# Modulation columns summed as a row and turned by transfers over HBM, residuals issued earlier, side work held back at group ends

## The chip, the cores and the metric

One core of a Trainium2 chip runs the whole kernel. The metric is the device time of one execution in microseconds. A core has a matrix engine (TensorE, PE in the profile), a vector engine (VectorE, DVE), an activation engine (ScalarE, ACT), GpSimd (POOL), and SyncE (SP), whose queue issues all the transfers of this kernel. Matmul results land in eight PSUM banks of 128 x 512 floats; everything else lives in SBUF, and HBM holds inputs and outputs.

## The reference

One layer of a decoder trunk on x (512 tokens x 1024), in float32: a modulation vector from c, two sparse attention mixers on a shared projection, a gated merge, an output projection, and a SwiGLU block.

```python
mod = jax.nn.silu(c) @ w_mod[l] + b_mod[l]
sh_m, sc_m, gt_m, sh_f, sc_f, gt_f = [m[:, None, :] for m in jnp.split(mod, N_MOD, axis=-1)]
h = rms_norm(x, g_mix_norm[l]) * (1.0 + sc_m) + sh_m
proj = h @ w_in[l]
...
o_a = dsa_attention(q_a, k_a, v_a, q_i, k_i, w_i)
...
o_b = moba_attention(q_b, k_b, v_b)
merged = (jax.nn.sigmoid(gate_a) * (o_a @ w_br_dsa[l])
          + jax.nn.sigmoid(gate_b) * (o_b @ w_br_moba[l]))
x = x + gt_m * (merged @ w_out[l])
h = rms_norm(x, g_ffn_norm[l]) * (1.0 + sc_f) + sh_f
g_ff, u_ff = jnp.split(h @ w_gate_up[l], 2, axis=-1)
x = x + gt_f * ((jax.nn.silu(g_ff) * u_ff) @ w_down[l])
```

The change concerns `sh_f` and `sc_f`, 1024 values each, which are needed with the channel on the partition (as columns), and the order of work around `x + gt_m * (merged @ w_out)`.

## The kernel before, in words

Every large product is done as three passes of a split weight and a split activation (high x high, high x low, low x high; `mm3`), so each weight tile `st` that arrives from HBM is cast by ACT to `wh`, and DVE forms `wl` = `st` - `wh`. Projections are done in groups: `group` cuts a 1024 x 512 weight block into four chunks; four PSUM banks (`psacc`) are filled over all chunks, and the last chunk's unit (`last`) goes bank by bank, so that each finished bank can be emptied (`fin`) while PE fills the others. These matmuls are the main work.

All else is side work: generators that are run between the main matmuls. It holds the norm, rotation and transposing of queries and keys (`post`), the index scores (`index_queries`: two matmuls per head into `pss` or `pspv`, a relu by ACT into a tile `s`, and DVE's weighing of it into `score`), the top-k rounds (`topk`), the attention heads (`head`), and the rest of the modulation vector (`columns_task`, `rows_task`, `gtf_task`).

No hardware decides the order. While the program is written out, `Clocks` keeps an estimated time for each engine and the time at which each tile is ready, from a cost formula. After each main triple, `main3` calls `step`, which advances each side task whose inputs are ready on these clocks and whose engines lead PE by less than the task's `slack`. The order so found is fixed in each engine's instruction stream, and every engine runs its stream strictly in order. For transfers, `arriving` sets a tile ready 2.0 after `ck.dma`, a running sum of transfer sizes that a transfer moves up only by its own size or to the tile's last use, not to the engines' present time. All operations are issued through one recorder (`Noted`), so the profile gives line 107 for all of them and tells them apart by tile names.

The second half of the modulation vector is made in `columns_task` (line 924): four parts of 512 columns, each by `mod_columns` (line 894). `column_sums` loads two 1 MB tiles `K` of `w_mod` and adds the eight row blocks, each times one column of silu(c), on DVE (`K<-K,cs`). `halves` splits the 128 x 512 sum into `gu` high (ACT) and low (DVE). Then the sum over partitions is taken on PE as eight matmuls that each move two columns of ones against a 128 x 128 block of the sums, so that it lands as columns, and DVE adds the bias from PSUM into `mcol` (lines 901 to 905). `mod_rows` (line 908) makes other parts as rows with two 512-column matmuls. `mcol` is first read at the end of `columns_task` and then in `norm_task`, past 400 us.

`out_units` (line 1111) does the second half of the output projection, token tile by token tile. After the last k of a tile, `main3` calls `step` before the residual (`s<-psacc,cg`, then `V<-V,s`) is issued and the bank is released. `merge` (line 981) joins the two gated branches. `prep` (line 522) casts a chunk's weights as soon as DVE's clock allows.

Of the kernel before, what the change touches and what calls it, by code (L numbers as in the profile page):

```python
# [25 lines left out]
P = 128  # L26
# [87 lines left out]
def layer(ctx, tc, x, vecs, w_mod, w_in, gvecs, w_br_dsa, w_br_moba, w_out, w_gate_up, w_down, cosh, sinh, cosi, sini, out):  # L114
# [6 lines left out]
    wp = ctx.enter_context(tc.tile_pool(name="wp", bufs=3))  # L121
    sm = ctx.enter_context(tc.tile_pool(name="sm", bufs=2))
    pp = ctx.enter_context(tc.tile_pool(name="pp", bufs=1, space=PS))

    NB = {"H": 4, "O": 4, "K": 4, "V": 2, "g": 16, "gu": 2, "s": 3, "pT": 2, "cg": 2}
    uid = [0]
# [15 lines left out]
    def done(*tiles):  # L142
        for tile in tiles:
            name = tile.tensor.name
            free[tag_of.pop(name)].append(ck.last[name][0])
# [12 lines left out]
    def ps(tag, shape=(P, 512), dt=F32):  # L158
        uid[0] += 1
        return taken("ps" + tag, pp.tile(list(shape), dt, name=f"ps{tag}_{uid[0]}", tag="ps" + tag, bufs=NPB[tag]))  # L160
# [266 lines left out]
    def room(tag, n=1):  # L427
        return lambda: sorted(free[tag])[n - 1] if len(free[tag]) >= n else None
# [9 lines left out]
    def spawn(gen, slack=2.0, rank=2, on=busy):  # L438
        tasks.append([gen, (), slack, on, rank])
        tasks.sort(key=lambda task: task[4])  # L440

    def step():

        moved = False
        while True:
            hit = False
            for wait in (0.0, 0.15):
                for task in list(tasks):
                    fill = task[4] == 3
                    if wait and (hit or not fill):  # L450
                        continue
                    while task in tasks:
                        now = ck.at[PE]
                        if max(ck.at[e] for e in task[3]) > now + task[2]:
                            break
                        limit = max(now, ck.at[DVE] + 0.12 + wait) if fill else now
                        if not all(w is not None and w <= limit for w in map(when, task[1])):
                            break
                        hit = True
                        try:  # L460
                            task[1] = next(task[0]) or ()
                            if not isinstance(task[1], tuple):
                                task[1] = (task[1],)
                        except StopIteration:
                            tasks.remove(task)
                        if fill:
                            break
            if not hit:
                return moved
            moved = True  # L470
# [21 lines left out]
    def group(srcs, n, accs_of, mm, order, fin, need=(), change=None):  # L492

        accs = {}
        nk = 2 * len(srcs)
        chunks = []
        for c, src in enumerate(srcs):
            def unit(w, ks, js, last, c=c):
                if not accs:
                    accs.update(accs_of())  # L500
                for a, b in ([(k, j) for j in js for k in ks] if last else [(k, j) for k in ks for j in js]):
                    mm(accs[b], w[0][:, a], w[1][:, a], 2 * c + a, b, c == 0 and a == 0, 2 * c + a == nk - 1)
                    if last and a == ks[-1]:
                        fin(b, accs[b])
                        done(accs[b])

            last = c == len(srcs) - 1
            h = (len(order) + 1) // 2
            parts = [((0, 1), order[:h]), ((0, 1), order[h:])] if last else [((0,), order), ((1,), order)]
            units = [lambda w, p=p, unit=unit, last=last: unit(w, p[0], p[1], last) for p in parts]  # L510
            chunks.append((lambda src=src, n=n: wload(src, 2, n), units, need, change))
        return chunks

    def drive(chunks, ws, ahead=2):
        sts = {}

        def load(c):
            if c < len(chunks) and chunks[c][0]:
                need_room("st")
                sts[c] = chunks[c][0]()  # L520

        def prep(c):
            if c < len(chunks) and chunks[c][0]:
                st = sts.pop(c)
                if chunks[c][3]:
                    chunks[c][3](st)
                uid[0] += 1
                h, l = [wp.tile(list(st.shape), F32R, name=f"w{q}_{uid[0]}", tag="w" + q) for q in "hl"]
                se.copy(h, st)
                yield h  # L530
                ve.tensor_tensor(out=l, in0=st, in1=h.bitcast(F32), op=ALU.subtract)
                done(st)
                ws[c] = h, l
            load(c + 1)

        load(ahead)
        for c, (load_of, units, need, _) in enumerate(chunks):
            pump(lambda: all(f in ready for f in need) and (not load_of or c in ws))
            for u, unit in enumerate(units):
                unit(ws.get(c))  # L540
                if u == 0:
                    spawn(prep(c + ahead), slack=4.0, rank=-1, on=(DVE,))
                    step()
            ws.pop(c, None)
# [339 lines left out]
    def halves(sums):  # L884

        yield room("gu", 2)
        hi, lo = (t("gu", [P, 512], F32R) for _ in range(2))
        yield sums
        se.copy(hi, sums)
        yield hi  # L890
        ve.tensor_tensor(out=lo, in0=sums, in1=hi.bitcast(F32), op=ALU.subtract)
        return hi, lo

    def mod_columns(col0):

        tile, sums = yield from column_sums(col0, "K")
        parts = yield from halves(sums)
        done(tile)
        yield parts + (room("pstr"),)
        pc = ps("tr", (P, 4, 2))  # L900
        for j in range(4):
            for n, part in enumerate(parts):
                te.matmul(pc[:, j, :], part[:, j * P:(j + 1) * P], oner.to_broadcast([P, 2]), start=n == 0, stop=n == 1)
        j0 = col0 // P
        ve.tensor_tensor(out=mcol[:, j0:j0 + 4], in0=pc[:, :, 0], in1=bm[:, j0:j0 + 4], op=ALU.add)
        done(pc, *parts)

    def mod_rows(acc, col0, tag):

# [57 lines left out]
    def br_done(br, half):  # L967
        def fin(f, acc):
            if not br and not half and not f:
                pump(lambda: len(free["K"]) == 4)  # L970
                merged.extend(t("K", [P, 4, S], F32R) for _ in range(4))
            j = 8 * br + 4 * half + f
            pump(lambda: f"gate{j}" in ready)
            ve.tensor_tensor(out=gates[j], in0=acc, in1=gates[j], op=ALU.mult)
            if not br:
                spawn(merge(half, f), slack=0.5, rank=0)
            if half and f == 3:
                done(*outs[br])
        return fin

    def merge(half, f):
        g, gb = gates[4 * half + f], gates[8 + 4 * half + f]
        ve.tensor_tensor(out=g, in0=g, in1=gb, op=ALU.add)
        yield g
        hi, lo = merged[half][:, f, :], merged[2 + half][:, f, :]
        se.copy(hi, g)
        yield hi
        ve.tensor_tensor(out=lo, in0=g, in1=hi.bitcast(F32), op=ALU.subtract)
        done(g, gb)
        ready.add(f"m{half}{f}")  # L990
        if all(f"m{a}{b}" in ready for a in range(2) for b in range(4)):
            ready.add("merged")
# [118 lines left out]
    def out_units():  # L1111
        units = []
        accs = {}
        for i in range(NT):
            for k2 in range(NK // 2):
                def unit(_, i=i, k2=k2):
                    if not i and not k2:
                        h2.extend(t("H", [P, 4, S], F32R) for _ in range(4))
                    if not k2:
                        need_room("psacc")  # L1120
                        accs[i] = ps("acc")
                    for k in (2 * k2, 2 * k2 + 1):
                        mh, ml = mk(k, i)
                        pump(lambda: len(wo) > k)
                        main3(accs[i], mh, ml, wo[k][0][:, 0], wo[k][1][:, 0], k == 0, k == NK - 1)
                    if k2 == NK // 2 - 1:
                        spawn(norm_task(i, residual(accs[i], gtm, i, 1)), slack=4.0, rank=-0.1 * i)
                        done(accs[i])
                        if i == NT - 1:
                            done(*gtm, *(q for hl in wo for q in hl), *merged)  # L1130
                units.append(unit)
        return units

# [198 lines left out]
```

## Time and profile before

| | |
|---|---|
| device time, three runs | 796.37, 797.54, 798.59 us (median 797.54) |
| profiled execution | 798.46 us |
| its span, first to last instruction | 796.4 us |
| instructions | 10056 |
| PE busy | 780.6 us, 98% |
| DVE busy | 475.6 us, 60% |
| ACT busy | 364.0 us, 46% |
| POOL busy | 28.4 us, 4% |
| HBM | 125 GB/s over the span |

Shares are of the span. An average over the whole span hides that DVE's and ACT's work lies mostly before 300 us. A row of a timeline gives start, duration, engine, operation, result <- operands, shape, count and, in brackets, the idle time ahead of it with what ended it. PE's durations overlap, since matmuls are pipelined: the time that one takes from the engine is the distance between starts, not the duration shown.

### The profile page before, as it was taken

The page shows a single profiled execution, that of the slowest core. Times are in us where ns is not written, and L with a number is a line of the kernel's source. Part 1 is how long each engine was busy: PE and PEld are TensorE (multiplying, and loading weights), DVE is VectorE, ACT ScalarE, POOL GpSimd, SP SyncE. Part 2 cuts the span into 40 slices and gives each one's busy share as a digit, 9 for nine tenths or more (in the row PEclk, how much of TensorE's full clock was granted, in tenths as well). Part 3 has the DMA queues.
Part 4 walks back from the last instruction along what each step waited for, and adds up shares of the span by engine and source line. Part 5 has one row for each costly group of instructions (what it writes and reads, how often), then busy time and mean ns, then how long its engine had stood idle before and what let it go on. Part 6 is the DMA issues. An engine that isn't in the chain of part 4 may idle for free.

```text
span 796.4 us, 10056 instructions
## 1 busy us (share of the span) xinstructions
PE 780.6 (98%) x3733; PEld 647.3 (81%) x3733; DVE 475.6 (60%) x873; ACT 364.0 (46%) x763; POOL 28.4 (4%) x32
## 2 busy tenths in 40 slices
PE   5999999999999999999999999999999999999998
PEld 4887788787788788888888988888888888888886
DVE  3974979998799638538857365333333333644542
ACT  5763579898566777334534323223322322211210
POOL 1000012110010000000000000000000000000000
PEclk8899999999999999999999999999999999999999
DMA  9946443321144444634520166332332322433411
GB/s 309 356 138 225 126 158 83 129 75 58 54 132 137 155 136 155 212 105 139 178 82 15 40 210 212 106 106 87 99 105 85 101 85 74 133 106 110 128 53 53
DMA packets 78036, 100.59 MB, mean 126 GB/s; under 512 B 5980, under 2 KB 46244, under 8 KB 77988
## 3 DMA queue, kind: packets, MB, share of 16 engines
q1 hardware_dynamic: 77988, 99.96, 39.7%
q8 instruction: 29, 0.48, 0.2%
q14 instruction: 19, 0.16, 0.1%
HBM read 97.85 MB, written 2.10 MB: 125 GB/s over the span
## 4 chain that ended last, share of the span: by engine, by line
PE 95%; ACT 2%; DVE 1%; DMA 1%; issue 0%; SPq 0%; POOL 0%; DVEq 0%; ACTq 0%
PE psacc L107 61%; PE pstr L107 16%; PE pspv L107 9%; PE pss L107 9%; DMA O<-in_x_dram 1%; ACT sqj L107 0%; ACT V L107 0%; DVE wl L107 0%; DVE score L107 0%; ACT g L107 0%; ACT s L107 0%; DVE O L107 0%; DVE pT L107 0%; DVE s L107 0%; POOL m L107 0%
## 5 line engine op out<-in xcount | busy, mean ns | idle before, releaser
L107 DVE TENSOR_TENSOR wl<-st,wh 128x1024 fp32r<-128x1024 f32 (+1 forms) x119 | 144.9, 1217 | 123.3 <-ACT wh L107 123.1
L107 ACT CAST wh<-st 128x1024 fp32r<-128x1024 f32 (+1 forms) x119 | 124.3, 1045 | 179.8 <-PE psacc L107 66.7
L107 PE MATMUL psacc<-H,wh 128*128 128x512 f32 x576 | 181.9, 397 | 0.0
L107 PE MATMUL psacc<-wh,H 128*128 128x512 f32 x384 | 131.1, 409 | 2.2 <-ACT H L107 1.3
L107 PEld LDWEIGHTS psacc<-H,wh 128*128 128x128 f32 x576 | 106.8, 188 | 23.0 <-issue 1.4
L107 PE MATMUL psacc<-H,wl 128*128 128x512 f32 x288 | 112.4, 390 | 0.0
L107 PEld LDWEIGHTS psacc<-wh,H 128*128 128x128 f32 x384 | 72.4, 189 | 19.4 <-ACT H L107 1.4
L107 PE MATMUL psacc<-wl,H 128*128 128x512 f32 x192 | 71.6, 394 | 0.0
L107 PEld LDWEIGHTS psacc<-H,wl 128*128 128x128 f32 x288 | 54.1, 188 | 11.5
L107 PE MATMUL pstr<-H,wh 128*128 128x512 f32 (+1 forms) x176 | 54.3, 390 | 0.0
L107 PEld LDWEIGHTS psacc<-wl,H 128*128 128x128 f32 x192 | 36.6, 191 | 7.7 <-issue 1.0
L107 POOL TENSOR_TENSOR m<-m,mhalf 128x4 f32<-128x4 f32 (+1 forms) x24 | 26.6, 1108 | 404.6 <-DVE m L107 357.0
L107 PE MATMUL psacc<-wh,K 128*128 128x512 f32 x128 | 39.8, 389 | 0.0
L107 PE MATMUL psacc<-O,wh 128*128 128x512 f32 x128 | 39.4, 389 | 0.0
L107 PEld LDWEIGHTS pstr<-H,wh 128*128 128x128 f32 (+1 forms) x176 | 32.3, 183 | 7.7
L107 ACT ACTIVATE s<-s,att 128x128 f32<-128x128 f32 (+3 forms) x64 | 34.1, 560 | 2.4 <-DVE att L107 2.4
L107 PE MATMUL pstr<-H,wl 128*128 128x512 f32 (+1 forms) x88 | 34.3, 390 | 0.0
L107 DVE TENSOR_TENSOR s<-psacc,s 128x512 f32<-128x512 f32 x12 | 8.3, 692 | 41.1 <-PE psacc L107 38.9
L107 PEld LDWEIGHTS psacc<-wh,K 128*128 128x128 f32 x128 | 24.0, 188 | 5.2 <-DVE g L107 0.2
L107 PEld LDWEIGHTS psacc<-O,wh 128*128 128x128 f32 x128 | 24.0, 188 | 5.0
L107 PEld LDWEIGHTS pspv<-pT,V 128*128 128x128 f32 x160 | 21.9, 190 | 6.4 <-DVE O L107 3.0
L107 DVE TENSOR_TENSOR st<-st,cg 128x1024 f32<-128x1024 f32 x22 | 26.8, 1219 | 0.0
(232 smaller groups left out, 1339.6 us busy)
## 6 DMA issues: line engine op xcount, KB each, us to landing
st<-in_w_gate_up_dram SPq DMA_DIRECT2D x88, 256.0 KB, 3.2
st<-in_w_in_dram SPq DMA_DIRECT2D x36, 512.0 KB, 3.6
K<-in_w_mod_dram SPq DMA_DIRECT2D x12, 1024.0 KB, 5.9
st<-in_w_down_dram SPq DMA_DIRECT2D x22, 512.0 KB, 3.6
K<-in_w_mod_dram SPq DMA_DIRECT2D x16, 512.0 KB, 6.2
st<-in_w_in_dram SPq DMA_DIRECT2D x16, 256.0 KB, 4.2
st<-in_w_mod_dram SPq DMA_DIRECT2D x8, 512.0 KB, 3.9
O<-in_x_dram SPq DMA_DIRECT2D x4, 512.0 KB, 5.4
```

The source lines that it names most:

```text
L107: inst = f(*args, **kw)
```

## The change

`mod_columns` takes the sum over partitions as a row: two matmuls with 512 moving columns and a two-column stationary of ones, a copy of the row by ACT into the sums' tile, a transfer of the row to HBM, a second transfer from there into four columns of `mcol`, and then the bias in place on DVE. `held_back` takes 1.0 from the lead that side work may have while the last chunk of a group is worked. `merge` gets a slack larger by 1.0. `prep` waits on the clocks for its load's planned arrival before the cast. In `out_units` the last triple of a token tile is no longer followed by `step`; that comes after the residual.

```diff
     def step():
...
-                        if max(ck.at[e] for e in task[3]) > now + task[2]:
+                        if max(ck.at[e] for e in task[3]) > now + task[2] - held_back[0]:
                             break
...
             def unit(w, ks, js, last, c=c):
                 if not accs:
                     accs.update(accs_of())
+
+                held_back[0] = 1.0 if last else 0.0
...
                 if chunks[c][3]:
                     chunks[c][3](st)
+                yield st
...
     def mod_columns(col0):

         tile, sums = yield from column_sums(col0, "K")
-        parts = yield from halves(sums)
+        hi, lo = yield from halves(sums)
+        yield hi, lo, room("pstr")
+        pc = ps("tr", (2, 512))
+        te.matmul(pc, oner.to_broadcast([P, 2]), hi, start=True, stop=False)
+        te.matmul(pc, oner.to_broadcast([P, 2]), lo, start=False, stop=True)
+        done(hi, lo)
+        yield pc
+        row = sums[0:1, :]
+        se.copy(row, pc[0:1, :])
+        done(pc)
+        yield sums
+        j0 = col0 // P
+        turned = dp.tile([1, 512], F32, name=f"turned{j0}")
+        nc.sync.dma_start(turned, row)
+        nc.sync.dma_start(mcol[:, j0:j0 + 4], turned.rearrange("o (a p) -> p (o a)", p=P), allow_slow_non_contiguous=True)
+        arriving(mcol, 512)
+        yield mcol
+        ve.tensor_tensor(out=mcol[:, j0:j0 + 4], in0=mcol[:, j0:j0 + 4], in1=bm[:, j0:j0 + 4], op=ALU.add)
         done(tile)
-        yield parts + (room("pstr"),)
-        pc = ps("tr", (P, 4, 2))
-        for j in range(4):
-            for n, part in enumerate(parts):
-                te.matmul(pc[:, j, :], part[:, j * P:(j + 1) * P], oner.to_broadcast([P, 2]), start=n == 0, stop=n == 1)
-        j0 = col0 // P
-        ve.tensor_tensor(out=mcol[:, j0:j0 + 4], in0=pc[:, :, 0], in1=bm[:, j0:j0 + 4], op=ALU.add)
-        done(pc, *parts)
...
-                spawn(merge(half, f), slack=0.5, rank=0)
+                spawn(merge(half, f), slack=1.5, rank=0)
...
-                        main3(accs[i], mh, ml, wo[k][0][:, 0], wo[k][1][:, 0], k == 0, k == NK - 1)
+
+                        (mm3 if k == NK - 1 else main3)(accs[i], mh, ml, wo[k][0][:, 0], wo[k][1][:, 0], k == 0, k == NK - 1)
                     if k2 == NK // 2 - 1:
                         spawn(norm_task(i, residual(accs[i], gtm, i, 1)), slack=4.0, rank=-0.1 * i)
                         done(accs[i])
                         if i == NT - 1:
                             done(*gtm, *(q for hl in wo for q in hl), *merged)
+                        step()
```

What this does to the streams is seen in three places. Numbers behind a name count allocations and differ between the kernels. On DVE, at the first of the four parts of the modulation columns, the stream of before is:

```order
L107 TENSOR_TENSOR wl_977<-st_941,wh_976 128x1024
L107 TENSOR_TENSOR gu_983<-K_858,gu_982 128x512
L107 TENSOR_TENSOR mcol<-pstr_1030,cols 128x4
L107 TENSOR_SCALAR score_991<-s_995,wi 128x256
L107 SCALAR_TENSOR_TENSOR score_991<-s_1000,wi,score_991 128x256
L107 TENSOR_TENSOR gu_1065<-g_663,cg_685 128x4x64 x2
```

and the stream of the change is:

```order
L107 TENSOR_TENSOR gu_1068<-K_855,gu_1067 128x512
L107 TENSOR_TENSOR wl_1074<-st_1032,wh_1073 128x1024
L107 SCALAR_TENSOR_TENSOR score_990<-s_1088,wi,score_990 128x256
L107 SCALAR_TENSOR_TENSOR score_990<-s_1094,wi,score_990 128x256
L107 TENSOR_TENSOR gu_1140<-g_667,cg_687 128x4x64 x2
L107 TENSOR_TENSOR mcol<-mcol,cols 128x4
L107 TENSOR_SCALAR K_1178<-K_1178,cs 128x512
L107 SCALAR_TENSOR_TENSOR K_1178<-K_1178,cs 128x512 x3
L107 SCALAR_TENSOR_TENSOR K_1180<-K_1180,cs,K_1178 128x512
L107 SCALAR_TENSOR_TENSOR K_1180<-K_1180,cs 128x512
L107 SCALAR_TENSOR_TENSOR score_990<-s_1127,wi,score_990 128x256
L107 SCALAR_TENSOR_TENSOR score_990<-s_1133,wi,score_990 128x256
```

The bias add now takes `mcol` itself, and behind it stand six products of the next part's sums and then the weighing of the next two index heads (`s_1127` and `s_1133`).

On ACT, around the row copy of the same part (the copy to one partition, `1x512`), the change has:

```order
L107 ACTIVATE g_665<-g_665,m_4_159_1025 128x128 x4
L107 ACTIVATE s_1127<-pss_1124 128x256
L107 ACTIVATE s_1133<-pspv_1130 128x256
L107 ACTIVATE sqj,m_4_180_1135<-g_667 128x128 x4
L107 COPY K_855<-pstr_1120 1x512
L107 COPY g_1150<-psacc_868 128x512
```

The relus of the two index heads and four squares of a norm stand ahead of it, and the emptying of the next group's first bank behind it.

On SP, the only queue that issues transfers, the change has at that place:

```order
L858 DMA K_1178<-in_w_mod_dram 128x4x512
L858 DMA K_1180<-in_w_mod_dram 128x4x512
L916 DMA turned_1174<-K_855 1x512
L180 DMA st_1305<-in_w_in_dram 128x2x512
L917 DMA mcol<-turned_1174 128x4x1
L180 DMA st_1371<-in_w_in_dram 128x2x512
```

A weight load now stands between the two new transfers, and the next weight load stands behind both.

On DVE, at the last token tile of the output projection (`s<-psacc,cg` is the residual's product, `V<-V,s` its sum, `pT<-pstr,acol,mcol` the modulation of a transposed token tile), before:

```order
L107 TENSOR_SCALAR pT_4142<-pstr_4137,acol,mcol 128x128 x4
L107 TENSOR_TENSOR s_4147<-psacc_4069,cg_3301 128x512
L107 TENSOR_TENSOR V_3116<-V_3116,s_4147 128x512
L107 TENSOR_TENSOR H_3934<-pT_4132,H_3932 128x4x128
L107 TENSOR_SCALAR m_1_801_4177<-ss_656 128x1
```

and in the change:

```order
L107 TENSOR_TENSOR s_4121<-psacc_4063,cg_3131 128x512
L107 TENSOR_TENSOR V_3242<-V_3242,s_4121 128x512
L107 TENSOR_SCALAR pT_4139<-pstr_4134,acol,mcol 128x128 x4
L107 TENSOR_SCALAR m_1_801_4172<-ss_658 128x1
L107 TENSOR_TENSOR H_3924<-pT_4129,H_3922 128x4x128
```

The residual, which releases the bank, now stands ahead of the four modulations.

## Rows read from the trace of the kernel before

**Rows 1.** The page, busy time of the engines over the span.

```profile
PE 780.6 (98%) x3733; PEld 647.3 (81%) x3733; DVE 475.6 (60%) x873; ACT 364.0 (46%) x763; POOL 28.4 (4%) x32
```

**Rows 2.** Waits of PE: us in total, times, longest.

```profile
PE psacc L107 <- DVE s L107: 1.0, 1, 1.0
PE psacc L107 <- ACT g L107: 0.8, 1, 0.8
```

**Rows 3.** Busy by stretch: length; PE, PEld, DVE, ACT, POOL, PEclk, DMA share, GB/s.

```profile
100.00:150.00 50.00, 49.96 (x262) 42.45 (x261) 45.28 (x94) 42.29 (x125) 10.53 (x7) 1.00 0.36 117
...
500.00:790.00 290.00, 290.00 (x1281) 240.15 (x1280) 113.23 (x112) 72.49 (x85) 0.00 (x0) 1.00 0.31 94
```

**Rows 4.** Timeline of PE: start, us, operation, around modulation matmuls.

```profile
107.34 1.15 PE L107 MATMUL pstr<-oner,gu 128*128 128x2 f32 x8
108.35 0.48 PE L107 MATMUL pspv<-O 128*128 128x256 f32 x2
...
159.01 1.03 PE L107 MATMUL pstr<-oner,gu 128*128 128x2 f32 x8
159.91 0.48 PE L107 MATMUL psacc<-wh,H 128*128 128x512 f32 x1
...
160.69 0.38 PE L107 MATMUL pss<-K,K 128*128 128x128 f32 x2
...
320.00 0.63 PE L107 MATMUL pstr<-gu,oner 128*128 128x512 f32 x2
320.47 0.62 PE L107 MATMUL psacc<-H,wh 128*128 128x512 f32 x2
```

**Rows 5.** Timeline of ACT and of PE where a bank copy is late.

```profile
151.83 1.30 ACT L107 ACTIVATE g<-g,m 128x128 f32<-128x128 f32 x4
153.01 0.62 ACT L107 CAST gu<-K 128x512 fp32r<-128x512 f32 x1
153.52 1.09 ACT L107 COPY g<-psacc 128x512 f32<-128x512 f32 x2
...
154.17 0.50 PE L107 MATMUL psacc<-wh,H 128*128 128x512 f32 x1 [0.75 <-ACT g L107]
```

**Rows 6.** Timeline of DVE and of PE where a residual is late.

```profile
429.37 1.37 DVE L107 TENSOR_SCALAR pT<-pstr,acol,mcol 128x128 f32<-128x128 f32 x4 [1.36 <-PE pstr L107]
...
431.39 1.81 PE L107 MATMUL psacc<-H,O 128*128 128x256 f32 x13 [0.99 <-DVE s L107]
```

**Rows 7.** Groups of ACT by shape: busy, mean ns.

```profile
L107 ACT ACTIVATE sqj<-g 128x128 f32<-128x128 f32 x64 | 19.9, 311 | 2.9 <-DVE m L107 1.3
...
L107 ACT ACTIVATION_READ_ACCUMULATOR sqj<-g 128x1 f32 x64 | 12.0, 188 | 0.0
```

**Rows 8.** DMA issues: KB each, median us to landing.

```profile
st<-in_w_in_dram SPq DMA_DIRECT2D x36, 512.0 KB, 3.6
...
st<-in_w_in_dram SPq DMA_DIRECT2D x1, 288.0 KB, 3.1
...
out_dram<-V SPq DMA_DIRECT2D x2, 128.0 KB, 1.7
```

**Rows 9.** Groups of DVE by shape: busy, mean ns.

```profile
L107 DVE TENSOR_TENSOR wl<-st,wh 128x1024 fp32r<-128x1024 f32 x118 | 144.1, 1221 | 123.3 <-ACT wh L107 123.1 <-DMA st<-in_w_in_dram 0.3
...
L107 DVE SCALAR_TENSOR_TENSOR K<-K,cs 128x512 f32<-128x512 f32 x24 | 17.9, 748 | 0.4
...
L107 DVE SCALAR_TENSOR_TENSOR score<-s,wi,score 128x256 f32<-128x256 f32 x7 | 3.4, 482 | 0.3
```

**Rows 10.** Waits of DVE between 80 and 440 us.

```profile
DVE mcol L107 <- PE pstr L107: 2.7, 4, 1.0
DVE cg L107 <- DMA cg<-in_vecs_dram: 1.8, 1, 1.8
```

**Rows 11.** Busy by stretch, the start of the span, columns as in Rows 3.

```profile
2.40:13.40 11.00, 4.85 (x26) 4.05 (x27) 4.29 (x12) 5.95 (x13) 2.25 (x5) 1.00 1.00 342
13.40:23.70 10.30, 8.99 (x36) 7.53 (x35) 5.78 (x15) 6.92 (x13) 0.00 (x0) 0.51 1.12 359
```

More of the change, by code (lines that the diff above doesn't have):

```diff
@@ L123, in layer @@
     pp = ctx.enter_context(tc.tile_pool(name="pp", bufs=1, space=PS))
+    dp = ctx.enter_context(tc.tile_pool(name="dp", bufs=1, space=bass.MemoryType.DRAM))
     NB = {"H": 4, "O": 4, "K": 4, "V": 2, "g": 16, "gu": 2, "s": 3, "pT": 2, "cg": 2}
@@ L440, in spawn @@
         tasks.sort(key=lambda task: task[4])
+    held_back = [0.0]
     def step():
```

## The prediction

> **What bounds the kernel now.** I read the busy times first: PE works 98% of the span [rows 1], so a time saved elsewhere counts only where PE would else wait, and a PE instruction saved counts in full. PE's waits on side work are short [rows 2]: one for a residual (1.0 us), one for a bank copy (0.8 us). The stretches then show where new waits could come from. From 500 us on PE runs 1281 matmuls in 290 us, 0.226 us each, with DVE busy for 113 us; between 100 and 150 us, where the first modulation columns are made, DVE is busy for 45.28 of 50 us and ACT for 42.29 [rows 3]. So a late DVE has some 4.7 us of idle time in 50 to catch up with, less in any one microsecond. Times below are against the profiled execution, 798.46 us (span 796.4 and 2.1 around it), which is 0.9 above the median 797.54.
>
> **The change part by part: gains.** The eight two-column matmuls of a modulation part took 1.01 us from one start to the next operation's start at 107.34, and 0.90 at 159.01; the pair of 512-column matmuls of `mod_rows`, the new form, took 0.47 at 320.00 [rows 4]. Four parts: 4 x (0.955 - 0.47) = **-1.9**.
>
> The residual: at 429.37 DVE starts four modulations, 1.37 us, and only then the residual that frees PE's next bank; PE idles for 0.99 us [rows 6]. With the residual first, the wait goes: its operands were there, and what is late next, the four modulations, feeds the same tile's H, far from the next matmul. With 0.1 for the slower first matmul behind a wait, **-1.1**.
>
> The smaller lead while a group is emptied: at 151.83 ACT does four scalings (1.18 to the next start) and a cast (0.51) ahead of the copy that frees a bank, and PE idles for 0.75 us [rows 5]. With less side work ahead, **-0.9** with 0.1 for the first matmul, which shows 0.50 there. No other PE wait has this form [rows 2]. The larger slack of `merge` restores its lead inside such groups, and the wait of `prep` for a planned arrival costs nothing: a weight load lands in 3.6 us [rows 8] and is issued two chunks ahead.
>
> **Losses.** Side matmuls now come in some 100 stretches between main ones instead of 92 (counted in PE's stream). Three main matmuls between side work took 0.78 us, 159.91 to 160.69 [rows 4], 0.10 more than three at 0.226. Eight more stretches: **+0.7** (0 to 0.8).
>
> **The wait of the bias add** is the largest term. DVE runs in order, and its add now waits for ACT's row copy and for two transfers in series, with six products and the index weighings queued behind it. Let X be the start of the first part's pair on PE. *Until the row is copied:* ACT does four scalings (1.18, as in [rows 5]), two relus of half a bank (0.4 each, from half the 0.54 per copy of [rows 5] and a start), four squares with their accumulator reads, 4 x (0.31 + 0.19) = 2.0 [rows 7], and the copy (0.54): X + 4.5. *The transfers, T:* the trace has none of 2 KB. The nearest are a store of 128 KB, 1.7 us, and a load in 288-byte pieces, 3.1 us [rows 8]; the second new transfer moves 512 pieces of four bytes. I take 1.7 + 3.1 = 4.8. At least it is 1.7 twice, 3.4. At most the second runs behind the weight load issued between them (3.6) and then takes its own 3.1: 6.7. The add comes at X + 9.3. *Behind it:* six products, at most 6 x 0.75 = 4.5; the first is a plain scaling, so I count 4.2; one weighing, 0.48 [rows 9]; then ACT's relu of the next head, 0.5, which needs the tile that this weighing frees; X + 14.5. The relu frees the PSUM bank of a later index matmul. *PE gets there at:* in its stream stand the pair (0.47), 36 main matmuls at 0.226 (8.1), and five index products of two matmuls each, three over 256 columns and two over 384, with four transposes (by columns at the same pace, 1.9): X + 10.5. PE waits for 4.0. Then the weight subtraction `wl` (1.22 [rows 9]) stands on DVE ahead of what the next heads need; I add 1.0 of it. **+5.0** (3.6 at T = 3.4, 6.9 at T = 6.7).
>
> By the Trainium skill, "DMA: Bandwidth & Descriptors", section "Anatomy of one DMA — SWDGE (gpsimd) path", every transfer has a fixed cost of about 2.0 us whatever its size; two in series make 4.0, an estimate from that page, by which this term would be 4.2, the next one 1.2, and the time below 800.1. The trace's own small store (1.7) lies near that figure, on another path than the page's.
>
> **Second part:** between the row copy and the add DVE has a `wl` (1.22) and two top-k scans (about 0.5 each): 2.2. It is late by T - 2.2 = 2.6. The next softmax, which frees a head's bank, stands behind the add, but top-k rounds, which nothing on PE awaits at once, stand there too; I take **+2.0** (0 to 4.5). **Third part:** some 12 us of other work stand between the row and the add: 0. **Fourth:** DVE has idle time there; **+0.3** (0 to 1).
>
> SP waits inside its queue for the row copy and for the first transfer to land, up to 5 us. Behind it stand weight loads that are cast some 10 us later, so this costs nothing; without that cover it would be what exceeds the slack, at most about 2.
>
> *Sum:* -1.9 - 1.1 - 0.9 + 0.7 + 5.0 + 2.0 + 0.3 = +4.1. 798.46 + 4.1 = 802.6; less 0.9, 801.7, **forecast 802.0**. The case's own range: with the low T, 3.6, 0.6 and 0, 798.8 (3.2 of net gains off); with the high one, 6.9, 4.5 and 1, 806.7. About 798.8 to 806.
>
> **The rivals.** *1. Faster: the wait falls where PE asks for nothing.* At the first part, PE loses only if DVE is later than PE's next need. The decisive point: counted from the row copy, T + 5.2 (products, weighing, relu) against the 6.0 us that PE has by the count above; ACT would have to copy earlier, or the streams to leave more main work between. For it: DVE once waited 1.8 us for a transfer (`cg<-in_vecs`) and PE's waits show nothing of it [rows 2, 10]; DVE has a tenth of idle time. Against it: even T = 3.4 fails by 2.6. Then only the gains stay: 798.46 - 3.2 - 0.9 = 794.4; the spread of three runs (2.2) puts 1.1 on either side, so from 793.3. I still give it 0.27, since what ACT has left to do at X is read from the streams alone.
>
> *2. No change: part of the wait reaches PE.* The first part costs 3.0 (low T, partly absorbed), the second none: 798.46 - 3.2 + 3.0 - 0.9 = 797.4. The chance covers 795.1 to 799.9; 0.18. Here too belongs that the change doesn't do what it says: `held_back` moves waits to other banks rather than removing them.
>
> *3. Slower still: PE's clock falls.* After a stretch in which PE was busy for 4.85 of 11 us, the next 10.3 us had a granted clock of 0.51, that is 1.2 GHz instead of 2.4 [rows 11]. If the 4 us wait brings that about, 10.3 us at 0.51 cost 5.0 more, half as long 2.5: 804 to 807. The skill's page "TensorE: Matmul & The Clock Gate", section "Part 1: The HAM clock gate", says that the throttled state is the default and activity releases it; the row agrees. Against it: the wait is shorter than the idle time in that stretch, 6 us. Chance 0.15.
>
> The main case has 0.40. About 0.3% (2.4 us) is what a measurement here can tell from no change: **faster 0.27** (rival 1), **same 0.18** (rival 2), **slower 0.55** (main case and rival 3). The range goes from 793.3 to 807: below it little of rival 1, above it the top of rival 3 and of the main case, together under 0.2.
>
> **What would show it.** Right: in the profile after, PE's waits hold an entry of 3 us or more some 10 us behind the first row pair, chained through ACT's relu to DVE's weighing, and DVE's waits an entry `mcol` released by a transfer, 3 to 7 us long; the waits of [rows 2] are gone; each pair takes 0.47. Wrong: the `mcol` waits are there and PE shows no new idle time (rival 1), or T is under 3 us, or the second transfer lands ahead of DVE's need.

## The result and the profile after

The change made the kernel slower: 806.36 us median of six runs (802.39 to 807.73) against 798.25 for six runs of before (796.37 to 799.24), a ratio of 1.0099 with a 95% interval of 1.0079 to 1.0119. Executions of one kernel fall into two groups some 2.5 to 3 us apart (23 of the kernel before in one session: 795.21 to 797.08 and 797.88 to 799.62), so small differences are read with their intervals. The direction was forecast and the range held the time, but the size was not: forecast +4.5 us, measured +8.1. The profiled execution took 807.73 us, with a span of 805.4, 9.0 longer than that of before.

The page of the changed kernel, busy times (to be read against [rows 1]):

```profile
PE 782.4 (97%) x3709; PEld 647.0 (80%) x3709; DVE 475.5 (59%) x873; ACT 365.0 (45%) x767; POOL 29.0 (4%) x32
```

No engine has much more to do than before: PE's busy time is 1.8 us longer with 24 matmuls fewer, ACT's 1.0, and DVE's is the same. The rest of the 9 us is in waits. PE's waits in the changed kernel (us in total, times, longest):

```profile
PE pss L107 <- DVE att L107: 5.4, 1, 5.4
PE pspv L107 <- ACT s L107: 3.1, 1, 3.1
...
PE psacc L107 <- DVE s L107: 0.7, 1, 0.7
```

The bank copy's wait of [rows 2] is gone, the residual's has become 0.7, and two new ones stand at the top. DVE's waits, in the same columns, have one that [rows 10] does not know:

```profile
DVE mcol L107 <- DMA mcol<-turned: 11.3, 2, 6.7
```

It comes twice, at the first and at the second of the four parts. The chain of the first part on three engines and SP's queue (timeline: start, duration, operation, in brackets the idle time ahead and what ended it):

```profile
113.84 0.62 PE L107 MATMUL pstr<-gu,oner 128*2 128x512 f32 x2
...
117.24 0.56 ACT L107 COPY K<-pstr 1x512 f32<-1x512 f32 x1
...
117.83 0.25 SPq L916 DMA_DIRECT2D turned<-K  x1
118.18 0.38 SPq L180 DMA_DIRECT2D st<-in_w_in_dram  x1
118.98 0.37 SPq L917 DMA_DIRECT2D mcol<-turned  x1
...
122.09 0.16 DVE L107 TENSOR_TENSOR mcol<-mcol,cols 128x4 f32<-128x4 f32 x1 [6.66 <-DMA mcol<-turned]
...
126.50 1.07 DVE L107 SCALAR_TENSOR_TENSOR score<-s,wi,score 128x256 f32<-128x256 f32 x2
...
127.08 0.49 ACT L107 ACTIVATE s<-pspv 128x384 f32<-128x384 f32 x1 [5.34 <-DVE score L107]
...
127.62 1.01 PE L107 MATMUL pspv<-O,O 128*128 128x384 f32 x2 [3.06 <-ACT s L107]
```

The row is copied by 117.80, the second transfer is issued 1.15 us after the first, the add runs 4.29 us after the copy, the six products are done by 126.5, the weighing frees the relu's tile, and PE, which was there at 124.56, starts at 127.62. The second part, on SP's queue and on DVE and PE:

```profile
161.07 0.24 SPq L916 DMA_DIRECT2D turned<-K  x1
164.46 0.37 SPq L180 DMA_DIRECT2D st<-in_w_in_dram  x1
164.88 1.45 SPq L917 DMA_DIRECT2D mcol<-turned  x1
...
163.22 1.22 DVE L107 TENSOR_TENSOR wl<-st,wh 128x1024 fp32r<-128x1024 f32 x1
164.36 0.88 DVE L107 MAX8 m<-score 128x8 f32<-128x256 f32 x2
169.85 0.16 DVE L107 TENSOR_TENSOR mcol<-mcol,cols 128x4 f32<-128x4 f32 x1 [4.62 <-DMA mcol<-turned]
...
176.74 0.80 PE L107 MATMUL pss<-K,K 128*128 128x128 f32 x2 [5.37 <-DVE att L107]
```

SP's wait for that load (line 180: us in total, times, longest), and the second transfer from issue to landing:

```profile
SPq L180 <- DVE m L107: 3.4, 1, 3.4
...
DMA to landing us min/median/max: 4.9/4.9/4.9
```

The second transfer is issued 3.8 us after the first, 2.7 later than at the first part. Between them stands a weight load, issued at 164.46, when DVE's `wl` (163.22, 1.22 long) has just finished with a buffer `st`: the load waited for that buffer, and the second transfer behind it. Then the second transfer takes 4.9 us to land, with the 512 KB load issued 0.4 us ahead of it; at the first part it took 3.1, with a load 0.8 ahead. From row copy (161.05) to add it takes 8.8 us. At the third and fourth parts DVE does not wait.

Behind both PE waits the granted clock is low. Stretches of the changed kernel (columns as in [rows 3]; the clock is the number after POOL's busy time):

```profile
127.62:130.60 2.98, 2.98 (x8) 2.49 (x9) 2.91 (x6) 0.82 (x3) 1.54 (x1) 0.50 0.00 0
130.60:134.00 3.40, 3.40 (x19) 2.81 (x18) 3.30 (x8) 3.26 (x8) 0.60 (x1) 0.99 0.56 154
...
176.74:181.60 4.86, 4.86 (x13) 3.89 (x14) 3.94 (x11) 2.21 (x6) 0.00 (x0) 0.50 0.39 108
```

2.98 and 4.86 us at 0.50 (1.2 GHz) cost 1.5 and 2.4 us. Waits and clock together: 3.1 + 5.4 + 1.5 + 2.4 = 12.4. Against that stand the pairs of row matmuls (0.46, 0.47, 0.46 and 1.00 us, 2.4 where the eight-matmul batches took 3.8) and the two waits of [rows 2] (1.1 of 1.8 gone): 12.4 - 1.4 - 1.1 = 9.9. The span grew by 9.0; the difference of 0.9 was not assigned.

### The profile page after: what moved, and what is told of

Same layout as the page of the kernel before. It is cut to its first block, busy times and chain, and to the rows that moved or that the text cites. A ratio compares the mean times of both kernels' runs of the same rounds, so it can differ in the third digit from the quotient of the medians.

```text
span 805.4 us, 10025 instructions
## 1 busy us (share of the span) xinstructions
PE 782.4 (97%) x3709; PEld 647.0 (80%) x3709; DVE 475.5 (59%) x873; ACT 365.0 (45%) x767; POOL 29.0 (4%) x32
## 4 chain that ended last, share of the span: by engine, by line
PE 86%; DVE 7%; DMA 3%; ACT 2%; issue 1%; SPq 0%; POOL 0%; DVEq 0%; ACTq 0%
PE psacc L107 54%; PE pstr L107 15%; PE pss L107 8%; PE pspv L107 8%; DVE score L107 2%; DVE g L107 1%; DMA mcol<-turned 1%; DVE wl L107 1%; DMA O<-in_x_dram 1%; DVE K L107 1%; DVE m L107 1%; DMA st<-in_w_gate_up_dram 1%; DMA st<-in_w_out_dram 1%; ACT sqj L107 0%; ACT g L107 0%
## 5 line engine op out<-in xcount | busy, mean ns | idle before, releaser
L107 PE MATMUL pss<-K,K 128*128 128x128 f32 (+3 forms) x64 | 23.6, 452 | 5.4 <-DVE att L107 5.4
```

The source lines that it names most:

```text
L107: inst = f(*args, **kw)
```

## The experiments

**A second profile of the change.** One execution, 803.71 us, shows whether those waits belong to the kernel.

> The change itself once more, for a second profile: its six runs lie between 802.4 and 807.7 us. Theory A: the first part's DVE wait (6.7 us) and the second's (4.6) are there again, PE waits behind both; if the time is lower, by shorter waits or a clock that did not fall. Rival: the waits of the first profile were one execution's chance, and the time is lost elsewhere.

Its PE waits:

```profile
PE pss L107 <- DVE att L107: 5.1, 1, 5.1
...
PE pspv L107 <- ACT s L107: 3.0, 1, 3.0
```

The same two waits are there, with 10.8 us on `mcol` in two waits and the clock at 0.97 and 0.93 over the stretches from 100 to 150 and from 150 to 200 us, as in the first profile. They belong to the program. The 4 us between the two executions lie elsewhere: the wait on the residual is absent here, and the first 50 us lost less (clock 0.93 against 0.90, PE's waits over 1 us shorter).

**The wait, and which part of the change brings it.** Three kernels: the change with only the planned arrival altered, the change without the row form, and the row form alone.

```diff
-        arriving(mcol, 512)
+        ck.ready[mcol.tensor.name] = (ck.ready[sums.tensor.name][0] + 10.0, None)
```

> The change with one line altered: the planner is told that the columns land 10 us after the row copy, so it places each bias add later. Theory A (DVE waits in order for the transfers, and this makes PE wait): the DVE waits on mcol (11.3 us in the change) and the PE waits of 5.4 and 3.1 us go, with the stretches at half clock behind them (1.5 and 2.4 us); 806.4 - 12.4 gives about 794. Theory B (the smaller lead and the other parts of the change cost the time): 804 to 806.

Measured: 793.70 us median against 796.16 for before, ratio 0.9972 (0.9959 to 0.9985). DVE has no wait on `mcol`, no PE wait behind the start is over 0.4 us, and the clock is 1.00 in every stretch from 100 us on:

```profile
PE pss L107 <- DVE att L107: 0.4, 1, 0.4
...
100.00:150.00 50.00, 50.00 (x254) 42.26 (x254) 43.76 (x93) 41.10 (x117) 7.84 (x6) 1.00 0.38 117
150.00:200.00 50.00, 49.78 (x252) 39.25 (x250) 42.16 (x126) 42.07 (x130) 5.44 (x5) 1.00 0.25 73
```

One number in the planner turns the change from 1% slower to 0.3% faster, with the same matmuls and the same transfers in another order. For `old_columns` the edit is the removed half of the diff of `mod_columns`, put back, and a guard in `prep` that waits until its load is issued.

> All of the change but the row form: the columns are made by the eight two-column matmuls as before. Theory A: no transfer, no wait; the gains of the other parts alone, 798.25 - 1.1 - 0.9 + 0.7, about 797. Theory B: 803 to 806.

Measured: 793.26 us, ratio 0.9965 (0.9950 to 0.9980): faster by 2.8 us, where 1.3 was counted. For `only_columns` the kernel before got the new `mod_columns` and nothing else.

> The kernel before with nothing but the row form and the two transfers. Theory A: -1.9 for the matmuls, and again a PE wait of 3 to 5 us at one or two of the four parts with the clock low behind it: 800 to 806. Theory B: 796.4, the matmuls' gain alone.

Measured: 805.20 us, ratio 1.0111 (1.0092 to 1.0129), in the range of theory A, but in smaller pieces than it said: no PE wait of 3 to 5 us, the longest is 2.2, and the clock falls behind that one alone. DVE waits for three of its parts, and the PE waits sit in other places than in the change, since the planner's order differs:

```profile
DVE mcol L107 <- DMA mcol<-turned: 12.0, 3, 6.0
...
PE pstr L107 <- DVE gu L107: 4.2, 3, 2.2
PE psacc L107 <- ACT g L107: 1.9, 2, 1.3
PE pspv L107 <- DVE O L107: 1.3, 1, 1.3
...
333.58 0.53 PE L107 MATMUL pstr<-gu,oner 128*128 128x512 f32 x1 [2.17 <-DVE gu L107]
...
333.90:337.30 3.40, 3.40 (x9) 2.62 (x8) 1.01 (x2) 1.04 (x1) 0.00 (x0) 0.50 0.49 138
```

So the row form alone is enough for the loss, and theory B falls. That the early placing of its adds is the reason is shown for the change, by `planned`; for this kernel it is the likely reading.

**SP's queue between the two transfers.** In `together` the next weight load is tied behind the second transfer. PE, DVE and ACT keep their order; on SP the load ahead of the first transfer goes behind the pair as well, at three of the four parts:

```diff
+            if prev:
+                with tc.issue_after(prev.ins):
+                    last_dma[0] = nc.sync.dma_start(st[:, :, o:o + n], ...)
...
-        nc.sync.dma_start(mcol[:, j0:j0 + 4], turned.rearrange(...), ...)
+        turn_dma[0] = nc.sync.dma_start(mcol[:, j0:j0 + 4], turned.rearrange(...), ...)
```

> The change, with the next weight load issued behind the second transfer instead of between the two; the streams of PE, DVE and ACT stay the same. Theory A1 (at the second part the weight load waits in SP's queue for a buffer that DVE frees only later, so that the second transfer is issued 3.8 us after the first): row copy to add falls from 8.8 to about 4.3 us at the second part, the PE wait of 5.4 us goes with its 2.4 us at half clock, the first part stays: about 798.5. Theory A2 (the transfers themselves take that long, or the load only delays them on the way): 804 to 806.

Measured: 797.48 us, ratio to before 1.0012 (0.9998 to 1.0026). On SP's queue and on DVE at the second part, and the second transfer's time to landing:

```profile
160.08 0.24 SPq L923 DMA_DIRECT2D turned<-K  x1
161.23 0.37 SPq L924 DMA_DIRECT2D mcol<-turned  x1
...
164.17 0.14 DVE L107 TENSOR_TENSOR mcol<-mcol,cols 128x4 f32<-128x4 f32 x1
...
DMA to landing us min/median/max: 2.1/2.1/2.1
```

The second transfer is issued as soon as the first has landed, 1.15 us on, and DVE finds its columns there. By the last row, it lands 2.1 us after its issue. The PE wait of 5.4 is 0.7. The first part stays, with a road shorter by 1.0 (the add at 121.11, with the row copied at 117.81 and no load ahead of the second transfer), and PE waits for 2.15 and 1.17 us there. Theory A1 holds: the load between the transfers is what made the road long, and without it the transfers take 3.3 us. The buffer is only half of the reason, though. Of the 5.5 us between 8.8 and 3.3, 2.7 are the later issue, the buffer's doing; 2.8 are the landing, 4.9 instead of 2.1, which is the second half of A2 (the load delays the transfer on the way). `together` takes both away at once; the rows, not the run, tell them apart.

**A longer road.** In `longer_road` the first part of `together` got one transfer more:

```diff
+        if j0 == 24:
+            again = dp.tile([1, 512], F32, name="again")
+            nc.sync.dma_start(again, turned)
+            turned = again
```

> The kernel 'together' with one more transfer, HBM to HBM, between the two of the first part; nothing else moves. In 'together' DVE waited for 5.7 us at that add and PE behind it for 3.3 us in two pieces. Theory A (PE's wait is the transfers' length less a fixed allowance): the road grows by some 1.5 to 2.5 us, PE's wait by as much, and the clock may fall behind it: 799 to 802. Rival (the wait is absorbed, or the transfers run beside something longer): 797.5.

Measured: 800.48 us, ratio 1.0033 (1.0019 to 1.0048). DVE's and PE's waits, and the stretch behind:

```profile
DVE mcol L107 <- DMA mcol<-again: 7.8, 1, 7.8
...
PE pspv L107 <- ACT s L107: 4.2, 1, 4.2
...
126.84:132.00 5.16, 5.16 (x14) 4.49 (x15) 4.99 (x10) 2.85 (x8) 2.14 (x1) 0.50 0.27 79
```

DVE waits 2.1 us longer, and the first piece of PE's wait grows by 2.1 (2.15 to 4.23): microsecond for microsecond. Then the clock is at 0.50 for 5.16 us, 2.6 us more; in `together` it stayed at 1.00 behind 2.15. The second piece of 1.17 does not come any more, since a slower PE arrives later. By these rows the kernel should lose 3.5 us against `together`; the ratios differ by 1.7 us and the medians by 3.0, with intervals that allow either.

**The clock's own share.** In `fill` PE gets matmuls by zero into the bank it is working on, right ahead of the two instructions that wait in the change:

```diff
+            nc.tensor.matmul(acc, zeros, rh, start=False, stop=False)
...
+            if (i, h) == (2, 2):
+                fill(12)
...
+        if (br, i, h) == (1, 0, 1):
+            fill(22)
```

> The change, with 12 and 22 matmuls by zero (2.7 and 5.0 us of PE's time) ahead of the two PE instructions that wait longest; all else in the same order. They add nothing to the sums and only keep PE at work while it would wait. Theory A (the idle time itself lets the clock fall, at a cost of 1.5 and 2.4 us): the stretches at 0.50 behind the waits go, 806.4 - 3.9 gives 802.5, a ratio to before of about 1.005. Rival (the clock costs nothing, or PE is held by the late results anyway): ratio 1.010 as for the change.

Measured: 801.82 us, ratio to before 1.0064 (1.0043 to 1.0084). PE does more work and the kernel is some 2.8 us faster than the change; the two intervals overlap at their ends, so the rows carry the reading. Stretches of `fill` behind the two places, its timeline of PE, its DVE waits on `mcol`, and SP's queue at the second part:

```profile
126.00:130.60 4.60, 3.43 (x19) 2.65 (x18) 4.45 (x10) 2.30 (x7) 2.14 (x1) 1.00 0.33 92
...
174.00:179.00 5.00, 5.00 (x28) 4.19 (x27) 4.58 (x18) 2.59 (x10) 0.00 (x0) 1.00 0.09 9
...
122.23 2.91 PE L168 MATMUL psacc<-wh,zeros 128*128 128x512 f32 x12
...
125.42 0.61 PE L107 MATMUL pspv<-O,O 128*128 128x384 f32 x2 [0.28 <-ACT s L107]
...
128.94 0.62 PE L107 MATMUL pspv<-O,O 128*128 128x384 f32 x2 [1.17 <-ACT s L107]
...
168.96 5.20 PE L168 MATMUL psacc<-wh,zeros 128*128 128x512 f32 x22
...
DVE mcol L107 <- DMA mcol<-turned: 6.5, 1, 6.5
...
158.87 0.24 SPq L930 DMA_DIRECT2D turned<-K  x1
160.02 0.37 SPq L931 DMA_DIRECT2D mcol<-turned  x1
```

The clock stays at 1.00. Of the 3.9 us that its fall cost, 1.17 come back as a second wait at 128.94, which the slow PE had covered: 2.7 is left, as measured.

The order did not stay the same everywhere, as the expectation says it would. PE (but for the added matmuls), ACT and DVE (but for making the zeros) keep theirs, but on SP one load has moved: the one between the two transfers of the second part now stands behind them. There DVE is not late, and the 22 matmuls fill no wait; they hold PE for 5.0 us (168.96 to 174.00) where it would idle for some 0.7, as in `together`. So the same wait, once idle and once filled, is compared at the first part alone. At the second part it is 5.4 us of idle time against 5.0 us of work. Unplanned, `fill` also repeats `together` with less moved: that one load out of the way, and DVE's wait at the second part is gone, with the second transfer landing in 2.2 us.

**The gains, one by one.** `held` is the kernel before with `held_back` and the slack of `merge`, and the guard of `old_columns`; `residual_first` is before with the `out_units` part of the diff.

> The kernel before with the smaller lead while a group's last chunk is worked, and the larger slack of merge, alone. Theory A: the PE wait on a bank copy (0.75 us) goes and one or two more of a few tenths; 0.5 to 1.5 us faster. If most of the 2.9 us that the change without the row form gains comes from here: 2 to 3 us faster.

> The kernel before with the residual issued ahead of the side work in the output projection, alone. Theory A: the PE wait of 1.0 us on the residual goes, 1.1 us faster and nothing else changes. If it is hidden: no change.

Measured: `held` 794.24 us, ratio 0.9966 (0.9951 to 0.9982), and `residual_first` 795.06 us, ratio 0.9980 (0.9964 to 0.9997), against 797.88. PE's waits in `held` that are not of the start:

```profile
PE psacc L107 <- DVE s L107: 1.0, 1, 1.0
PE psacc L107 <- ACT g L107: 0.3, 1, 0.3
```

In `held` the bank copy's wait fell from 0.8 to 0.3, and two of 0.2 us that before had (on `O` and on `V`) are gone: 0.9 us of its 2.7 (by the interval 1.4 to 3.9). Where the rest comes from stays open; no wait shows it. In `residual_first` the wait of 1.0 is gone, and its gain of 1.6 us (0.2 to 2.9) covers the 1.1 counted.

**A shorter plan.** `planned_4us` has 4.0 in place of 10.0, and the guard.

> As 'planned', but the planner is told 4 us from row copy to columns, the length of the road where nothing stands between the transfers, instead of 10. In SP's order two weight loads now stand between the two transfers of the first part. Theory A1 (a load between them waits for a buffer that DVE frees, and the second transfer with it): the first part's road is 6 us or more, DVE waits for 2 us or more there, and PE too where it has no cover: 795 to 801. Theory A2 (only the transfers' own time counts): no wait on mcol over 1 us, 794.

Measured: 793.53 us, ratio 0.9952 (0.9932 to 0.9972). SP's queue and DVE at the first part, and DVE's waits:

```profile
115.40 0.25 SPq L918 DMA_DIRECT2D turned<-K  x1
115.75 3.19 SPq L180 DMA_DIRECT2D st<-in_w_in_dram  x2
118.99 0.46 SPq L919 DMA_DIRECT2D mcol<-turned  x1
...
122.36 0.16 DVE L107 TENSOR_TENSOR mcol<-mcol,cols 128x4 f32<-128x4 f32 x1 [1.92 <-DMA mcol<-turned]
...
DVE mcol L107 <- DMA mcol<-turned: 5.0, 3, 2.2
```

Half of theory A1's forecast came: with two loads between the transfers the road is 7.0 us (3.6 to the second issue, 3.4 from there to the add) and DVE waits for 1.9. The other half missed: PE shows no wait over 0.2 us at any of the three places, though DVE waited for up to 2.2. There a few microseconds of work do stand between DVE's add and PE's need. This version and `old_columns` beat both kernels; their intervals overlap, and neither is shown to be the better.

## Why the prediction was right or wrong

**The gains.** The row matmuls: predicted -1.9, measured -1.4 in the change, since the fourth pair waited for half a microsecond between its two matmuls. The residual: its wait was 0.7 in one profile and absent in the other; alone it brought 1.6 us against the 1.1 counted, within its interval. The smaller lead: counted at -0.9, with +0.7 for more switching between main and side matmuls; together they bring -2.7. This step was too small by 2.5 (by the interval, 1.2 to 3.7). It took the two waits of [rows 2] for all that PE lost; the smaller ones make 0.4 of it, and the rest stays open.

**The first part of the modulation columns.** The working was right, step by step: row copied at X + 4.0 (X + 4.5 counted), road 4.3 us (4.8), add at X + 8.3 (X + 9.3), relu done at X + 13.7 (X + 14.5), PE there at X + 10.7 (X + 10.5), wait 3.1 (4.0). One count in it is off: the index products and transposes, put at 1.9 "at the same pace", make 1.6 by that pace (3584 columns at 0.226 us for 512) and took 2.1. The further +1.0 was not seen in the change but stands in `fill` and `together` as 1.17; in the change the slow clock hid it. The road stands between its bounds. By the estimate from the Trainium skill, "DMA: Bandwidth & Descriptors", section "Anatomy of one DMA — SWDGE (gpsimd) path", it would have been 4.0; the runs show 3.3 with nothing between the transfers, 4.3 with a load between them, and 8.8 at the second part, where that load also waited.

**The second part is the step that failed.** Predicted: road 4.8, bounds 3.4 to 6.7, DVE late by 2.6, PE by 2.0, and SP's blocking at nothing. Measured: road 8.8, DVE late by 4.6, PE by 5.4. The upper bound took the weight load between the two transfers for a transfer of 3.6 us that slows the second one. That happened: the second transfer took 4.9 us to land, against 2.1 with no load ahead. But the load is an instruction in SP's stream first, which waits for a buffer that DVE frees; the second transfer stood behind that wait, 2.7 us, and DVE behind the second transfer. Without these 2.7 the road would be 6.1, inside the bounds. The order fence of SP showed the load there. The prediction asked what waits behind the new transfers, and not what the instruction between them waits for. `together` and `fill`, which move that load away, remove the delay.

DVE's cover was mis-sized the other way, and by luck that helped: 2.2 us of work between row copy and add were counted, but DVE worked until 165.23, 4.2 us after the copy (two passes over `g` besides the `wl` and the scans). With 2.2 it would have been late by 6.6.

PE's share of DVE's delay was mis-sized as well: 2.0 of 2.6 was taken, since top-k rounds stand behind the add. They absorb nothing. From the add (169.85) to the softmax that frees PE's bank (176.39) DVE does 6.5 us of work in its fixed order, and a delay ahead of it goes through whole: 4.6 us, on top of the 0.7 that PE waits there in `together`, where DVE is not late.

**Third and fourth parts.** Counted at 0 and +0.3; DVE did not wait at either.

**The clock.** It stood as a rival of its own, with 0.15 and a price of 2.5 to 5.0 us. It fell in both profiles of the change and in `longer_road`, and cost 3.9 us, 2.7 net of a wait that it covered. The mechanism was right; that the price came out inside its bounds is partly luck, since two falls of 1.5 and 2.4 us made it and one was meant. The place in the sum was wrong: the fall is no other case but a follower of the main one, which put it at nothing. What spoke against it, that the wait is shorter than the 6 us of idle time in [rows 11], did not hold: 3.06 us were enough, and in `only_columns` 2.17. That row is no measure anyway. In its first stretch, printed at 1.00, matmuls of 128 columns start 0.21 us apart at 7.66 and 0.11 apart at 11.70, so PE was at the low level for part of it. The Trainium skill, "TensorE: Matmul & The Clock Gate", section "Part 1: The HAM clock gate", says that activity releases the throttle; `fill`, where PE stayed at work, agrees with its 1.00.

**The losses by terms.** First part 5.0 counted, 3.1 measured; second 2.0 and 5.4; third and fourth 0.3 and 0; the clock 0 and 3.9: together 7.3 and 12.4. The rest of the sum came out some 1.1 us lower than counted (8.1 less 12.4 is -4.3, against -3.2), which hid that much of the difference.

**The rivals.** Rival 1, the faster case, did not happen in the change, for the reason given, that PE's need comes too early in the stream; it came true where the planner was told of a longer road (`planned`, 0.9972: 2.2 us faster than before, where 3.2 were worked out). Rival 2 did not happen: `together` (1.0012) is what it looks like.

## What to carry to other kernels

When an instruction order is fixed by a planner's clocks, a new transfer chain needs a true arrival time there: an in-order engine that is sent to the result early stops all that is queued behind it, and here 11 us of such waiting came with 12 us lost, in waits and clock, on an engine that never touched the transfers. For a chain of transfers on a shared queue, read what stands between its links, what that waits for, and how much it moves: here a load in between held the second link back by 2.7 us and made its landing 2.8 us longer. And a wait of the matrix engine of some microseconds is to be priced with the low clock that may follow it.

## What the runs showed of the hardware

A transfer of 2 KB from SBUF to HBM was followed by the next one, which waited for its landing, 1.15 us after its issue. With a 1 MB load issued 0.3 us behind it, it was 3.5 us (325.67 to 329.15 in `only_columns`). One of 2 KB from HBM to HBM took 1.89 us by the same measure (117.10 to 118.99 in `longer_road`). The second new transfer, 512 pieces of four bytes from HBM into SBUF, took 2.1 us from issue to the add that waited for it with nothing just ahead of it in the queue, 3.1 with a 512 KB load issued 0.8 us earlier, 4.9 with one issued 0.4 us earlier (4.6 in the second profile, 3.3 in `planned_4us`), and 4.9 in `only_columns` with a 1 MB load issued 0.85 us earlier. With nothing ahead, the form that looks worst, four bytes a piece, cost less than a 288 KB load's 3.1 [rows 8]; most of its longer times came with a load just ahead.

PE's granted clock was 0.50 behind waits of 3.06 and 5.37 us in the change, of 3.0 and 5.1 in its second profile, and of 4.23 in `longer_road`, for about 3 to 5 us each time, and behind one of 2.17 in `only_columns`, for 3.4 us; behind 2.15 us, and 1.17 soon after, in `together` it was 1.00. The length of the wait alone does not tell whether the clock falls.
